# A decoder layer on one core: the opening reordered in halves, with x stored to DRAM later

## The chip, the cores and the metric

The kernel runs on one core of a Trainium2 chip, as one program of some 51,000 instructions. Its time is the device time of one execution in microseconds (us). A core has five engines that run their own instruction streams: TensorE (PE in the profile, with PEld for its weight loads), VectorE (DVE), ScalarE (ACT), GpSimd (POOL) and SyncE (SP). SP computes nothing; its queue, and POOL's, hold the instructions that start transfers between DRAM and the on-chip memory. Each engine takes its instructions in order, and one that waits holds up those behind it. Results of TensorE go to banks of PSUM, from where VectorE or ScalarE read them.

## The reference

One layer (DEPTH is 1) of a decoder over 1024 prompt rows and 8 x 4 sample rows, 1056 rows of 1024 values, all f32. A conditioning vector c for each of nine sequences (the prompt and eight samples) gives nine model vectors of 1024, three for each sublayer: shift, scale and gate.

```python
mod = jax.nn.silu(c) @ ada_w + ada_b                       # ada_w: 1024 x 9216
sh1, sc1, gt1, sh2, sc2, gt2, sh3, sc3, gt3 = jnp.split(mod, 9, axis=-1)
h = rms_norm(x, norm_ffn1) * (1 + sc1) + sh1
a, b = split(h @ ffn1_w_in, 2)                             # ffn1_w_in: 1024 x 5632
x = x + 0.5 * gt1 * ((silu(a) * b) @ ffn1_w_out)           # first FFN, D_FF = 2816
h = rms_norm(x, norm_mix) * (1 + sc2) + sh2
x = x + gt2 * token_mixer(h)                               # two branches: attention, retention
h = rms_norm(x, norm_ffn2) * (1 + sc3) + sh3
x = x + 0.5 * gt3 * swiglu_ffn2(h)
y = rms_norm(x, norm_final)
```

What the first FFN needs before its first product: x, transposed, and two of the nine vectors, sc1 (vector 1) and sh1 (vector 0).

## The kernel before

**Layout.** Activations are held transposed, 128 values of the model dimension to a tile and rows along it: X is 8 tiles (k = 0 to 7) by 1056 columns. The columns are worked in three row blocks of 352 (`rb` 0, 1, 2). Products are made with f32 accuracy from two rounded parts: `split` writes a high part with ScalarE (L183) and the remainder with VectorE (L193), and `mm3` makes three matmuls for each k (high by high, high by low, low by high: L242, L243, L244). One output tile for one row block, a `unit`, is thus 24 matmuls of 352 columns; a pair of units (`pa`, `pb`) makes one tile of the gated FFN.

**Weights.** A `W` pool has `raw` buffers of 512 KB for loads (`wr`, asked for on SP at L211) and `parts` pairs of buffers for the split parts. `w` (2 raw, 4 pairs) serves the FFN; `w0` (4 raw, 2 pairs) serves the model vectors in the opening, and a small pool of one each serves the other seven vectors, done beside the FFN (`more`).

**Model vectors.** `ada` makes vectors in the order it is given. A vector is made in halves of 512 (`u`), a half from four pieces of 256 x 512 of `ada_w` (`kq`; in the trace their tiles are `ada_0` to `ada_3`, the numbers of vector and half being left out). With the condition vectors as the stationary operand PE makes 18 (or 9) x 512 results in `adap`; ScalarE copies them to `ab` (L420), one matmul with `pick` or the identity turns them (L390), and VectorE adds the bias and makes the scale (L393, L395). Vector 1 (the scale) is marked `whole`: its pieces go to PE as plain f32, without a split. Vector 0 (the shift) and the rest are split.

**The opening**, in program order: the identity and constants; on SP the tables `cm` and `pgt`, the seven vectors of `vec` (bias and gains) and the conditions `c9`; their transposes; the four lambda vectors `lv` and the lambda of the attention; x by nine blocks of rows, each loaded by POOL's queue into `xn` (3 buffers, L751), transposed by eight PE transposes (L756) and copied to X by ScalarE and VectorE (L757); the sum of squares of row block 0; vector 1, then vector 0; and then the norm of row block 0, which writes `hh` and `hl`, the two parts of h, for k = 0 to 7 (L456, L460 to L465). Only then the first FFN: `ffn_plain` works three tile pairs in the order (tile 0, rb 0), (1, 0), (0, 1), (1, 1), (0, 2), (1, 2), (2, 0..2), with the norm of row block 1 traced after (0, 0), and `entry` after (0, 1): the norm of row block 2 and, by `keep1`, three stores of X to `xd` in DRAM, on POOL's queue (L769). After that the memory of X is given to the sums of a seven-product scheme (`sums`, L519 on), in which the other 19 tile pairs run (`ffn_seven`); X is read back from `xd` much later.

**Who orders.** The program order is not the order on the engines. A planner takes the traced instructions and issues on each engine the earliest in program order that is ready by its own estimates of time, and the result is fixed in the program. So a load whose buffer is free, or a store whose columns are written, can go out far ahead of its place. `step` ties the PE part of side work behind the last matmul traced.

Of the kernel before, what the change touches and what calls it, by code (L numbers as in the profile page):

```python
# [20 lines left out]
P = 128  # L21
# [84 lines left out]
def build(tc, i):  # L106
# [41 lines left out]
    def aux_ps(name):  # L148
        return banks[0][1].tile([P, 512], F32, tag="aux", name=name, bufs=banks[0][3])
# [132 lines left out]

    vT = cp.tile([P, 113], F32, name="vT")
    cs = cp.tile([P, KT, 18], F32R, name="cs")
    csf = cp.tile([P, KT, 9], F32, name="csf")
    with tc.tile_pool(name="init", bufs=1) as ip:
        vec = ip.tile([P, P], F32, name="vec")
        o = 0
        for n, r in (("ada_b", 72), ("norm_ffn1", 8), ("norm_mix", 8), ("norm_ffn2", 8), ("norm_final", 8),
                     ("ret_norm_g", 8), ("subln_g", 1)):  # L290
            src = i[n] if n == "norm_final" else i[n][0]
            ld(out=vec[o:o + r, :], in_=src.rearrange("(r p) -> r p", p=P))
            o += r
        pv = aux_ps("pv")
        T.transpose(pv[:, :113], vec[:113, :], ident[:113, :113])
        V.tensor_copy(out=vT[:], in_=pv[:, :113])
        c9 = ip.tile([9, D], F32, name="c9")
        ld(out=c9[0:1, :], in_=i["c_prompt"])
        ld(out=c9[1:9, :], in_=i["c_sample"])
        pc = aux_ps("pc")  # L300
        for k in range(KT):
            T.transpose(pc[:, k * 16:k * 16 + 9], c9[:, k * P:(k + 1) * P], ident[:9, :9])
        S.activation(csf[:], pc[:, :128].rearrange("p (k v) -> p k v", v=16)[:, :, :9], AF.Silu)
        split(cs[:, :, 0:9], cs[:, :, 9:18], csf[:])
    gff1, gmix, gff2, gfin, gret = (vT[:, 72 + 8 * j:80 + 8 * j] for j in range(5))
    subg = cp.tile([P, 1], F32, name="subg")
    V.tensor_scalar(out=subg[:], in0=vT[:, 112:113], scalar1=(1.0 - LAM_INIT) * 0.5, scalar2=None, op0=ALU.mult)
    retg = cp.tile([P, KT], F32, name="retg")
    V.tensor_scalar(out=retg[:], in0=gret, scalar1=0.25, scalar2=None, op0=ALU.mult)

    nlam = cp.tile([P, 1], F32, name="nlam")
    with tc.tile_pool(name="lam", bufs=1) as lp:
        lv = lp.tile([P, 4, 64], F32, name="lv")
        for j, n in enumerate(("lam_q1", "lam_k1", "lam_q2", "lam_k2")):
            ld(out=lv[:, j, :], in_=i[n][0].partition_broadcast(P))
# [11 lines left out]
    rsq = pool(root, "rsq")  # L327
# [50 lines left out]
    def ada(w, vectors):  # L378


        todo = [(v, u, kq) for v in vectors for u in range(2) for kq in range(4)]

        def load(n):
            (j, _, _, whole), u, kq = todo[n]
            c0 = j * D + u * 512
            return (w.load if whole else w.get)(i["ada_w"][0][kq * 256:(kq + 1) * 256, c0:c0 + 512], 2, 512, f"ada{j}_{u}_{kq}")

        def finish(pa, j, kind, g, whole, u):
            pt, t = pa[:, 512:], mods[j]
            T.matmul(pt[:, :36], ab[:], quarter(0) if whole else pick[:], start=True, stop=True)  # L390
# [9 lines left out]

        nxt, ready = load(0), None
        yield
        for n, ((j, kind, g, whole), u, kq) in enumerate(todo):
            if ready:
                finish(*ready)
                ready = None
            if kq == 0:
                m = 9 if whole else 18
                if u == 0:
                    mods[j] = (xp if j < 5 else cp).tile([P, KT, 9], F32, name=f"mod{j}")  # L410
                pa = big_ps(f"adap{j}_{u}")
            for k in range(2):
                for q, ww in enumerate((nxt,) if whole else nxt):
                    T.matmul(pa[:m, :512], (csf if whole else cs)[:, kq * 2 + k, :], ww[:, k, :],
                             start=(kq == 0 and k == 0 and q == 0), stop=(kq == 3 and k == 1 and (whole or q == 1)))
            if n + 1 < len(todo):
                nxt = load(n + 1)
            if kq == 3:
                for q in range(4):
                    S.copy(out=ab[32 * q:32 * q + m, :], in_=pa[:m, q * P:(q + 1) * P])  # L420
                ready = (pa, j, kind, g, whole, u)
            yield
# [15 lines left out]
    def norm(tp, X, rb, mods, gs, sh, tt=None):  # L438
# [14 lines left out]
        for k in range(KT):  # L453
            t = (tt or tp).tile([P, RB], F32, tag="t", name=f"nt{rb}_{k}", bufs=4)
# [29 lines left out]
    def ffn_plain(w, tp, win, fts, lead, pre, back=iter(()), more=iter(()), quiet=0):  # L484


        ws = {}
        for q, rb in [(q, rb) for q0 in range(0, len(fts), lead) for rb in range(NRB)
                      for q in range(q0, min(q0 + lead, len(fts)))]:
            ft = fts[q]  # L490
            if rb == 0:
                ws[q] = (w.get(win[:, ft * P:(ft + 1) * P], 8, P, f"wa{ft}"),
                         w.get(win[:, DFF + ft * P:DFF + (ft + 1) * P], 8, P, f"wb{ft}"))
            pa = unit(ws[q][0], rb, f"pa{ft}_{rb}")
            pb = unit(ws[q][1], rb, f"pb{ft}_{rb}")
# [235 lines left out]
    lower = ExitStack()  # L731
    w = W(lower, 2, 4)
    bridge = []
    with ExitStack() as sc, ExitStack() as sb_:
# [8 lines left out]
        tp = pool(sc, "t1")  # L743
        with ExitStack() as s2:
            xq = pool(s2, "xn")
            w0 = W(s2, 4, 2)
            for rt in range(9):
# [3 lines left out]
                st(out=xn[:n, :], in_=src)  # L751
                for hf in range(2):
                    pt = mm_ps(f"xt{rt}_{hf}")
                    for q in range(4):
# [4 lines left out]
            todo = norm(tn, X, 0, mods, 1, 0, tp)  # L759
            next(todo)  # L760
            run(ada(w0, [(1, "scale", gff1, True), (0, "shift", None, False)]))
            run(todo)
        w2 = W(sc, 1, 1)

        more = ada(w2, [(2, "half", None, False), (4, "scale", gmix, False), (3, "shift", None, False), (5, "gate", None, False),
                        (7, "scale", gff2, False), (6, "shift", None, False), (8, "half", None, False)])

# [25 lines left out]
        win1 = i["ffn1_w_in"][0]  # L793
        todo = back()
        ffn_plain(w, tp, win1, [0, 1, 2], LEAD, {(0, 0): norm(tn, X, 1, mods, 1, 0, tp), (PQ, 1): entry()}, todo, more, LEAD)
# [868 lines left out]
```

## Time and profile before

| | us |
|---|---|
| median of 3 executions | 3089.32 |
| the three | 3077.48, 3091.77, 3089.32 |
| the profiled execution, its own time | 3076.16 |
| its span in the profile | 3074.4 |
| granted TensorE clock, mean over the span | 0.987 |
| PE busy over the span | 2955.1 |

The profile is one execution. Each row of it names an engine, a line of the kernel, an operation and the tiles out<-in, with a start, a duration and, in brackets, how long the engine stood before it and what released it. Rows with xN are N instructions merged. A PE row's duration includes its run through the array, so following matmuls overlap, and a busy PE is not a PE at its peak. SPq and POOLq rows, and POOL rows with DMA, are the issue of a transfer, not the transfer. The DMA share is that of 16 engines.

### The profile page before, as it was taken

What the parts mean: (1) busy time and instruction counts of PE and PEld (TensorE: products, weight loads), DVE (VectorE), ACT (ScalarE), POOL (GpSimd) and SP (SyncE); (2) the same over time, 40 slices, a digit from 0 to 9 for tenths busy, and PEclk for the clock granted to TensorE, in tenths of its full rate; (3) what the DMA queues carried; (4) which work ended last, traced back from release to release, by engine and by line L of the source; (5) the groups of instructions that cost most, each with busy time, mean ns of one, the idle gap of its engine ahead of it and who ended that gap; (6) DMA issues with size and microseconds to landing.
All of it is one profiled execution on the core that took longest, in us unless ns stands there. A gap on an engine that the chain in (4) does not pass through costs nothing.

```text
span 3074.4 us, 51401 instructions
## 1 busy us (share of the span) xinstructions
PE 2955.1 (96%) x20167; PEld 2827.7 (92%) x20167; DVE 1969.2 (64%) x3823; ACT 1319.1 (43%) x2580; POOL 544.1 (18%) x722
## 2 busy tenths in 40 slices
PE   6999999999999999999999999998999999999998
PEld 2999999999999999988899998997898999999997
DVE  4875665665556666657666777676659655556546
ACT  5554444422234243336555555554545433333212
POOL 2200000000132322313233332332023000000002
PEclk8999999999999999999999999999999999999998
DMA  7143334653131322223222221225651222226311
GB/s 280 52 135 118 121 119 120 205 168 117 59 98 63 103 73 89 84 70 119 64 63 71 66 76 58 83 74 173 208 156 40 88 74 84 77 74 221 103 51 57
DMA packets 278732, 319.29 MB, mean 104 GB/s; under 512 B 15568, under 2 KB 224049, under 8 KB 278490
## 3 DMA queue, kind: packets, MB, share of 16 engines
q1 hardware_dynamic: 253418, 232.83, 24.9%
q0 software_dynamic: 25072, 83.18, 7.3%
q8 instruction: 158, 2.59, 0.3%
q14 instruction: 84, 0.69, 0.1%
HBM read 240.00 MB, written 75.96 MB: 103 GB/s over the span
## 4 chain that ended last, share of the span: by engine, by line
PE 35%; DVE 7%; issue 4%; ACT 3%; DMA 3%; POOL 1%; SPq 0%; DVEq 0%; ACTq 0%; POOLq 0%
PE po L244 3%; PE po L242 3%; PE po L243 3%; PE x L242 2%; PE x L243 2%; PE x L244 2%; PE q L243 1%; PE q L242 1%; PE q L244 1%; PE gp L242 1%; PE gp L244 1%; PE gp L243 1%; ACT P L1331 1%; DVE mx L1329 1%; DMA m<-md 1%
## 5 line engine op out<-in xcount | busy, mean ns | idle before, releaser
L242 PE MATMUL x<-hh,c 128*128 128x264 f32 x624 | 177.7, 285 | 3.3 <-DVE p L616 1.4
L242 PE MATMUL x<-gh,c 128*128 128x264 f32 x624 | 178.3, 286 | 0.6 <-ACT u L612 0.6
L193 DVE TENSOR_TENSOR c<-s,c 128x512 fp32r<-128x512 f32 x156 | 107.6, 690 | 111.1 <-ACT c L183 107.0
L243 PE MATMUL x<-hl,c 128*128 128x264 f32 x624 | 177.8, 285 | 0.3 <-DVE hl L193 0.3
L243 PE MATMUL x<-gl,c 128*128 128x264 f32 x624 | 177.7, 285 | 0.0
L244 PE MATMUL x<-hh,c 128*128 128x264 f32 x624 | 176.8, 284 | 0.8 <-DVE c L193 0.8
L244 PE MATMUL x<-gh,c 128*128 128x264 f32 x624 | 177.3, 284 | 0.0
L1331 ACT ACTIVATE P<-s,mx 128x256 f32<-128x256 f32 (+7 forms) x128 | 94.2, 739 | 136.7 <-DVE mx L1329 130.1
L475 DVE SCALAR_TENSOR_TENSOR Z<-po,mod,Z 128x352 f32<-128x352 f32 (+3 forms) x176 | 96.5, 554 | 87.3 <-PE po L244 86.6
L475 DVE SCALAR_TENSOR_TENSOR X<-po,mod,X 128x352 f32<-128x352 f32 (+3 forms) x152 | 82.0, 549 | 85.6 <-PE po L244 85.5
L625 POOL DMA_DIRECT2D gd<-p x39 | 21.1, 542 | 614.8 <-DVE p L620 614.8
L183 ACT ACTIVATE c<-s 128x512 fp32r<-128x512 f32 x156 | 97.5, 626 | 70.2 <-issue 35.1
L242 PEld LDWEIGHTS x<-hh,c 128*128 128x128 f32 x624 | 117.4, 188 | 4.7 <-DVE p L616 1.6
L242 PEld LDWEIGHTS x<-gh,c 128*128 128x128 f32 x624 | 117.4, 188 | 3.3 <-ACT u L612 0.9
L244 PEld LDWEIGHTS x<-hh,c 128*128 128x128 f32 x624 | 117.4, 188 | 1.2 <-DVE c L193 1.0
L243 PEld LDWEIGHTS x<-gl,c 128*128 128x128 f32 x624 | 117.3, 188 | 0.9
L243 PEld LDWEIGHTS x<-hl,c 128*128 128x128 f32 x624 | 117.4, 188 | 0.6 <-DVE hl L193 0.5
L244 PEld LDWEIGHTS x<-gh,c 128*128 128x128 f32 x624 | 117.4, 188 | 0.2
L242 PE MATMUL po<-hh,wo_1h 128*128 128x352 f32 (+1 forms) x328 | 105.7, 323 | 0.0
L243 PE MATMUL po<-hl,wo_1h 128*128 128x352 f32 (+1 forms) x328 | 104.2, 318 | 0.0
L244 PE MATMUL po<-hh,wo_1l 128*128 128x352 f32 (+1 forms) x328 | 103.8, 318 | 0.0
L242 PE MATMUL po<-hh,wo_0h 128*128 128x352 f32 (+1 forms) x328 | 103.5, 316 | 0.0
(1445 smaller groups left out, 11122.2 us busy)
## 6 DMA issues: line engine op xcount, KB each, us to landing
gr<-gd SPq DMA_DIRECT2D x40, 528.0 KB
gd<-u POOLq DMA_DIRECT2D x39, 264.0 KB, 2.3
gd<-p POOLq DMA_DIRECT2D x39, 264.0 KB, 2.3
ada_0r<-ada_w SPq DMA_DIRECT2D x18, 512.0 KB
ada_1r<-ada_w SPq DMA_DIRECT2D x18, 512.0 KB
ada_2r<-ada_w SPq DMA_DIRECT2D x18, 512.0 KB
ada_3r<-ada_w SPq DMA_DIRECT2D x18, 512.0 KB
st<-state_ret SPq DMA_DIRECT2D x32, 256.0 KB
```

The source lines that it names most:

```text
L183: S.activation(out, in_, AF.Copy, scale=scale)
L193: (eng or V).tensor_tensor(out=l, in0=src, in1=f(h), op=ALU.subtract)
L242: T.matmul(out, wh, xh, start=first and j == 0, stop=False, **kw)
L243: T.matmul(out, wh, xl, start=False, stop=False, **kw)
L244: behind[0] = T.matmul(out, wl_, xh, start=False, stop=last and j == n - 1, **kw).ins
L475: V.scalar_tensor_tensor(out=x[k][:, c0:c0 + n], in0=p_[:, :n], scalar=gt[:, k, 0:1], in1=x[k][:, c0:c0 + n], op0=ALU.mult, op1=ALU.add)
L625: st(out=gd[ft][:, :HR], in_=p1[:])
L1329: V.tensor_reduce(out=mx[:, :n], in_=sv[:, :, :wd], op=ALU.max, axis=AX.X, negate=True)
L1331: S.activation(pr[c][:, :wd], sv[:, j, :wd], AF.Exp, bias=mx[:, j:j + 1], accum_out=sums[c][:, qb:qb + 1])
```

## The change

The opening is cut and reordered; the FFN and everything behind it keep their order.

- `c9`, the conditions, is loaded first; then `first()` starts the generator of the model vectors, which asks for four pieces of `ada_w`; only then come the seven vectors and `cm`. `pgt` and the lambda part move into `lambdas`, run behind the FFN's pair (1, 0).
- Vectors 1 and 0 are made by halves: first half of 1, first half of 0, then the two second halves. All 16 pieces are split; `whole` is gone.
- x comes in three parts: rows 0 to 2 before the model vectors, by POOL's queue as before; rows 3 to 5 after the first half of the norm, by SP's queue; rows 6 to 8 behind the pair (1, 0), by SP's queue.
- The norm of row block 0 stops at k = 4. The first pair's first 12 + 12 matmuls (k = 0 to 3) are traced between its halves, the first weight pair (`wa0`, `wb0`) just before.
- The three stores of X to `xd` are issued by SP's queue instead of POOL's; their place in the program, in `entry`, stays.

The core of the diff:

```diff
-    ld(out=cm[:], in_=i["t_main"][:, :C_N0])
...
-    ld(out=pgt[:], in_=i["page_table"].rearrange("b n -> (b n)").unsqueeze(0))
...
+    lower = ExitStack()
+    w = W(lower, 2, 4)
+    sc, s2 = ExitStack(), ExitStack()
+    tp = pool(sc, "t1")
+    xq = pool(s2, "xn")
+    w0 = W(s2, 4, 2)
+
+    def opening(first):
+        with tc.tile_pool(name="init", bufs=1, side="right") as ip:
+            c9 = ip.tile([9, D], F32, name="c9")
+            ld(out=c9[0:1, :], in_=i["c_prompt"])
+            ld(out=c9[1:9, :], in_=i["c_sample"])
+            first()
+            vec = ip.tile([P, P], F32, name="vec")
...
+            ld(out=cm[:], in_=i["t_main"][:, :C_N0])
...
+    def lambdas():
+        ld(out=pgt[:], in_=i["page_table"].rearrange("b n -> (b n)").unsqueeze(0))
+        lp = pool(sc, "lam")
...
-    def ada(w, vectors):
-        todo = [(v, u, kq) for v in vectors for u in range(2) for kq in range(4)]
+    def ada(w, vectors, halves_first=False, ahead=0):
+        todo = [(v, u, kq) for v, u in ([(v, u) for u in range(2) for v in vectors] if halves_first else
+                                        [(v, u) for v in vectors for u in range(2)]) for kq in range(4)]
+        raws = {}
+        def load(n, part=True):
...
+            if n not in raws:
+                raws[n] = w.load(i["ada_w"][0][kq * 256:(kq + 1) * 256, c0:c0 + 512], 2, 512, name)
+            if part:
+                h, l = w.out(2, 512, name)
+                split(h[:], l[:], raws.pop(n)[:], eng=w.eng)
+                return h, l
...
+        for n in range(ahead):
+            load(n, False)
         nxt, ready = load(0), None
...
         for k in range(KT):
+            if halves and k == 4:
+                yield
...
-            for rt in range(9):
-                st(out=xn[:n, :], in_=src)
-            run(ada(w0, [(1, "scale", gff1, True), (0, "shift", None, False)]))
+        a0 = ada(w0, [(1, "scale", gff1), (0, "shift", None)], True, 4)
+        opening(lambda: next(a0))
...
+        run(rows_in(range(3), st, mm_ps))
+        todo = norm(tn, X, 0, mods, 1, 0, tp, True)
+        next(todo)
+        for _ in range(8):
+            next(a0)
+        got = {0: gated(w, win1, 0)}
+        next(a0)
+        next(todo)
+        begun = {(0, 0): units(got[0], 0, 0)}
+        for u in begun[0, 0]:
+            next(u)
+        run(rows_in(range(3, 6), ld, aux_ps))
+        run(a0)
+        run(todo)
+        def rest_in():
+            yield from rows_in(range(6, 9), ld, aux_ps)
+            s2.close()
+            lambdas()
...
             for rb in range(NRB):
-                keep1(X, rb, st)
+                keep1(X, rb, ld)
...
-        ffn_plain(w, tp, win1, [0, 1, 2], LEAD, {(0, 0): norm(tn, X, 1, mods, 1, 0, tp), (PQ, 1): entry()}, todo, more, LEAD)
+        ffn_plain(w, tp, win1, [0, 1, 2], LEAD, {(0, 0): norm(tn, X, 1, mods, 1, 0, tp), (1, 0): rest_in(), (PQ, 1): entry()},
+                  todo, more, LEAD, begun, got)
```

`rows_in` is the old loop over blocks of rows with the queue and the PSUM pool as arguments; `gated` and `units` are the old loads and units of a tile pair; `later` delays the pool and the generator of the other seven vectors until they are first stepped.

More of the change, by code (lines that the diff above doesn't have):

```diff
@@ L285, in build @@
     csf = cp.tile([P, KT, 9], F32, name="csf")
[L286 to L304, printed above, removed]
@@ L305, in build @@
-    gff1, gmix, gff2, gfin, gret = (vT[:, 72 + 8 * j:80 + 8 * j] for j in range(5))
[L306 to L312, printed above, removed]
+    subg = cp.tile([P, 1], F32, name="subg")
@@ L375, in quarter, with finish @@
         return ident[:].rearrange("p (q x) -> p q x", x=32)[:, :, o:o + 9]
-    def ada(w, vectors):
-        todo = [(v, u, kq) for v in vectors for u in range(2) for kq in range(4)]
[L383 to L388, printed above, removed]
+    def ada(w, vectors, halves_first=False, ahead=0):
[3 more added lines that the diff above has]
+        def load(n, part=True):
+            (j, _, _), u, kq = todo[n]
+            c0, name = j * D + u * 512, f"ada{j}_{u}_{kq}"
+            if n not in raws:
[4 more added lines that the diff above has]
+                return h, l
+        def finish(pa, j, kind, g, u):
             pt, t = pa[:, 512:], mods[j]
-            T.matmul(pt[:, :36], ab[:], quarter(0) if whole else pick[:], start=True, stop=True)
+            T.matmul(pt[:, :36], ab[:], pick[:], start=True, stop=True)
             tv = t[:, 4 * u:4 * u + 4, :]
@@ L399, in finish @@
                 V.tensor_scalar(out=tv, in0=tv, scalar1=0.5, scalar2=None, op0=ALU.mult)
+        for n in range(ahead):
+            load(n, False)
         nxt, ready = load(0), None
         yield
-        for n, ((j, kind, g, whole), u, kq) in enumerate(todo):
+        for n, ((j, kind, g), u, kq) in enumerate(todo):
             if ready:
@@ L412, in ada @@
             for k in range(2):
-                for q, ww in enumerate((nxt,) if whole else nxt):
-                    T.matmul(pa[:m, :512], (csf if whole else cs)[:, kq * 2 + k, :], ww[:, k, :],
-                             start=(kq == 0 and k == 0 and q == 0), stop=(kq == 3 and k == 1 and (whole or q == 1)))
+                for q, ww in enumerate(nxt):
+                    T.matmul(pa[:18, :512], cs[:, kq * 2 + k, :], ww[:, k, :],
+                             start=(kq == 0 and k == 0 and q == 0), stop=(kq == 3 and k == 1 and q == 1))
             if n + 1 < len(todo):
@@ L419, in ada @@
                 for q in range(4):
-                    S.copy(out=ab[32 * q:32 * q + m, :], in_=pa[:m, q * P:(q + 1) * P])
-                ready = (pa, j, kind, g, whole, u)
+                    S.copy(out=ab[32 * q:32 * q + 18, :], in_=pa[:18, q * P:(q + 1) * P])
+                ready = (pa, j, kind, g, u)
             yield
@@ L490, in ffn_plain @@
             ft = fts[q]
[L491 to L495, printed above, removed]
+            if rb == 0 and q not in ws:
+                ws[q] = gated(w, win, ft)
+            pa, pb = (run(u) for u in begun.get((q, rb)) or units(ws[q], ft, rb))
             for _ in range((q, rb) == (quiet - 1, 2) if q < quiet else 2 - rb % 2):
@@ L742, in build, with rows_in @@
         tn = pool(xs1, "n1", side="right")
[L743 to L746, printed above, removed]
-            for rt in range(9):
+        def rows_in(rts, eng, ps):
+            for rt in rts:
                 n = P if rt < 8 else NS
@@ L758, in build, with later @@
                                                       in_=pt[:].rearrange("p (k c) -> p k c", c=P)[:, :, :n])
-            todo = norm(tn, X, 0, mods, 1, 0, tp)
-            next(todo)
-            run(ada(w0, [(1, "scale", gff1, True), (0, "shift", None, False)]))
[L762 to L766, printed above, removed]
+                yield
+        win1 = i["ffn1_w_in"][0]
+        run(rows_in(range(3), st, mm_ps))
[16 more added lines that the diff above has]
+            lambdas()
+        def later():
+            yield from ada(W(sc, 1, 1), [(2, "half", None), (4, "scale", gmix), (3, "shift", None), (5, "gate", None),
+                                         (7, "scale", gff2), (6, "shift", None), (8, "half", None)])
+        more = later()
         def keep1(X, rb, eng):
```

40 lines of the change are left out of this document (30 added, 10 removed).

## The prediction

> **What bounds the kernel now.** I read the busy totals first, then the same totals by stretches of the span, then the opening in order of time, on SP's queue and on the engines that it feeds.
>
> The page's first part:
>
> ```profile
> PE 2955.1 (96%) x20167; PEld 2827.7 (92%) x20167; DVE 1969.2 (64%) x3823; ACT 1319.1 (43%) x2580; POOL 544.1 (18%) x722
> ```
>
> Busy time by stretch (us and count of PE, PEld, DVE, ACT, POOL; granted clock; DMA share; GB/s):
>
> ```profile
> 0.00:80.00 80.00, 51.12 (x185) 24.34 (x185) 39.26 (x61) 40.35 (x77) 20.14 (x29) 0.87 0.76 269
> 80.00:180.00 100.00, 96.93 (x618) 90.35 (x618) 90.18 (x145) 52.85 (x92) 16.21 (x19) 1.00 0.25 76
> ...
> 180.00:3074.00 2894.00, 2807.08 (x19368) 2712.98 (x19367) 1839.74 (x3619) 1225.91 (x2412) 507.75 (x674) 0.99 0.32 100
> ```
>
> TensorE bounds the kernel as a whole, and nothing in the change touches what it does after the opening. In the first 80 us it is short of work: 29 us idle, and 185 matmuls where the next 100 us hold 618. So the change is worth what it takes off the opening, less what comes back between 80 and 180 us, where VectorE has only 100 - 90.18 = 9.8 us free.
>
> What the opening waits for, in stretches of 5 us (same columns):
>
> ```profile
> 0.00:5.00 5.00, 0.00 (x0) 0.00 (x0) 0.50 (x3) 1.28 (x1) 2.44 (x9) 1.00 0.50 143
> ...
> 10.00:15.00 5.00, 5.00 (x21) 2.94 (x22) 1.05 (x3) 0.98 (x3) 0.53 (x1) 1.00 0.33 116
> ...
> 45.00:50.00 5.00, 4.79 (x12) 0.82 (x9) 2.82 (x7) 2.43 (x4) 0.43 (x1) 1.00 1.07 403
> 50.00:55.00 5.00, 0.00 (x0) 0.00 (x0) 2.56 (x3) 1.62 (x4) 0.49 (x1) 0.91 1.04 403
> 55.00:60.00 5.00, 3.64 (x8) 1.75 (x9) 3.77 (x6) 3.20 (x8) 1.39 (x2) 0.50 0.61 158
> ...
> 70.00:75.00 5.00, 5.00 (x14) 2.45 (x13) 3.04 (x5) 2.46 (x4) 0.00 (x0) 0.54 0.00 1
> ```
>
> The transfers are the limit: at 45 to 55 us they run at 403 GB/s, all 16 engines busy, while PE has nothing from 50 to 55. There is a hole early (116 GB/s at 10 to 15 us). Its cause stands on SP's queue, and the stores of x, which nobody needs yet, on POOL's (start, duration):
>
> ```profile
> 6.14 0.47 SPq L211 DMA_DIRECT2D ada_1r<-ada_w  x1
> 10.91 0.35 SPq L315 DMA_DIRECT2D lv<-lam_q  x1
> ...
> 12.72 0.43 SPq L211 DMA_DIRECT2D ada_2r<-ada_w  x1
> ...
> 28.50 0.96 POOL L769 DMA_DIRECT2D xd<-X  x1
> ...
> 34.21 0.91 POOL L769 DMA_DIRECT2D xd<-X  x1
> ...
> 42.07 0.91 POOL L769 DMA_DIRECT2D xd<-X  x1
> ...
> 79.64 0.20 DVE L393 TENSOR_TENSOR mod<-adap,vT 128x36 f32<-128x36 f32 x1 [1.15 <-PE adap L390]
> ...
> 83.27 0.43 PE L243 MATMUL pa<-hl,wa0h 128*128 128x352 f32 x1 [0.25 <-DVE hl L465]
> 83.53 0.33 PE L244 MATMUL pa<-hh,wa0l 128*128 128x352 f32 x1
> 83.69 0.32 PE L242 MATMUL pa<-hh,wa0h 128*128 128x352 f32 x1
> ```
>
> SP stood from 6.61 to 10.91 us before the lambda vectors, with two ada pieces behind them. The last of the four halves of the two model vectors is ready at 79.64 + 0.20 = 79.84 us, and from 83.3 us PE runs unbroken, a matmul every 0.16 us. I call the first moment M; the sum is about where M goes.
>
> **The change part by part.** (1) *Bytes ahead of M.* From the DMA part of the trace, sizes and counts of the opening:
>
> ```profile
> xd<-X POOLq DMA_DIRECT2D x3, 1408.0 KB, 9.6
> xn<-x_prompt POOLq DMA_DIRECT2D x8, 512.0 KB, 6.5
> ...
> wa0r<-ffn_w_in SPq DMA_DIRECT2D x1, 512.0 KB
> ...
> xn<-x_sample POOLq DMA_DIRECT2D x1, 128.0 KB, 5.4
> ```
>
> Before M lie 16 ada pieces (8 for each vector, 512 KB as the others), x with 8 x 512 + 128, four w pieces of 512, and about 106 KB of small vectors: 8192 + 4224 + 2048 + 106 = 14570 KB = 14.9 MB. The three stores are 4224 KB = 4.3 MB more. The first 5 us moved 143 x 5 = 0.72 MB, which at 403 GB/s is 1.8 us, so transfers start in effect at 3.2 us. With the stores behind M the last piece lands at 3.2 + 14.9 / 0.403 = 40.2 us; with all of them ahead, at 3.2 + 19.2 / 0.403 = 50.8 us. The change puts the conditions and four ada pieces ahead of the seven vectors and moves pgt and the lambda loads far back, so I count the early hole as closed.
>
> By "DMA: Bandwidth & Descriptors" of the Trainium skill (section Bandwidth, Where 436 GB/s comes from) loads from HBM are held to about 358 GB/s for a core, not 403; as an estimate from that figure the two landings would be 44.9 and 56.8 us, each 5 to 6 us later than above. This trace's 403 over 10 us, with loads and stores mixed, is above it, and I keep 403.
>
> From landing to M the trace has the last piece of before, and a buffer's turn:
>
> ```profile
> 44.67 0.37 SPq L211 DMA_DIRECT2D ada_0r<-ada_w  x1
> ...
> 53.35 1.06 ACT L183 ACTIVATE ada_0h<-ada_0r 128x1024 fp32r<-128x1024 f32 x1 [3.49 <-DMA ada_0r<-ada_w]
> ...
> 54.44 1.23 DVE L193 TENSOR_TENSOR ada_0l<-ada_0r,ada_0h 128x1024 fp32r<-128x1024 f32 x1 [2.44 <-ACT ada_0h L183]
> 55.70 0.37 SPq L211 DMA_DIRECT2D ada_0r<-ada_w  x1
> ...
> 73.59 1.06 ACT L183 ACTIVATE ada_3h<-ada_3r 128x1024 fp32r<-128x1024 f32 x1 [0.70 <-PE adap L414]
> ...
> 74.68 1.23 DVE L193 TENSOR_TENSOR ada_3l<-ada_3r,ada_3h 128x1024 fp32r<-128x1024 f32 x1 [0.53 <-ACT ada_3h L183]
> ```
>
> The last split starts at 73.59, M is at 79.84: 6.25 us. So M by bytes is 46.4 us (stores behind) to 57.1 us (stores ahead).
>
> (2) *Slots.* The ada loads still have four raw buffers. One was issued at 44.67, its data was there at 53.35, its split ended at 55.67, and the buffer was asked for again at 55.70: 11.0 us a turn. Now all 16 pieces go through splits, four turns. The first ends about when four pieces and half as much x have landed and been split, 3.2 + 3.7 / 0.403 + 2.3 = 14.7 us; three more turns give 47.7, and from a split's end (74.68 + 1.23 = 75.91) to M is 3.9: M = 51.6 us. The turn was measured under full transfers, so it is no floor and no ceiling.
>
> I take M = 52, near the slots' value, since the stores' place is open: they went out on POOL as soon as their columns were there, long ahead of their line in the program, and SP's queue is ordered by the same planner. Gain at M: 79.84 - 52 = 28 us; ends 33 and 23.
>
> (3) *Eight more splits.* The scale vector's eight pieces went to PE as plain f32. Now each costs ACT 1.06 and DVE 1.23 us: ACT +8.5, DVE +9.8. DVE's work up to M becomes 39.3 + 9.8 = 49.1 us, to be done between about 8 us (the first piece, 0.5 MB from 3.2 us on at half the rate with x beside it, lands near 6, and ACT's half comes first) and 52, in 44 us. It worked at 39.3 of 80 before. Taking 75% of the 44 us, 33 are done and 16 go behind M; at 90% it is 9.5, at 60% 22.7. That is not all urgent (squares and copies of later rows, the second weight pair). Behind M, DVE has the 9.8 us free, most of it in one wait for PE that such work can fill:
>
> ```profile
> 100.72 0.52 DVE L500 TENSOR_TENSOR silu<-silu,pb 128x352 f32<-128x352 f32 x1 [6.37 <-PE pb L244]
> ```
>
> So 16 - 9.8 = 6 us come back as stalls of PE (0 to 13 at the ends). From M on the order of the FFN is the old one.
>
> (4) *First half before the second.* Blocks k 0 to 3 of the first row block and their 24 matmuls may run while the second halves load. Before, PE had also done scattered matmuls of that kind by 83 us (it took them out of order from 73 us on), so I count nothing; at most 24 matmuls more are ahead, 3.8 us of gain.
>
> (5) *At nothing.* The 16 f32 matmuls become 32 split ones on a PE that idles 29 us here; if they did bind, M would move past 52 and that is inside the 57. x rows 3 to 8 go from POOL's to SP's queue and their transposes into the idle PE. If the 24 transposes of rows 6 to 8 fell behind M they would be on PE's path, by the group below 24 x 0.309 = 7 us at most. The seven vectors and the eps columns come after four ada pieces, still long before the first mod result of any half needs them; if they were late, that result would be late by as much. The lambda part's Exp sits in the FFN then: two table loads at worst, 1.28 us each, on an ACT that is busy 52.85 of 100 us. POOL loses nine issues; nobody waits for them. The stores must have read X before the sums overwrite it (113 us before): even issued at the first row block's end, about 72, they need 4.3 / 0.403 = 10.7 us, done by 83 against 113 - 28 = 85, with DMA at share 0.04 then.
>
> ```profile
> L756 PE MATMUL xt<-ident,xn 128*128 128x128 f32 (+1 forms) x72 | 11.4, 309 | 4.4 <-DMA xn<-x_prompt 2.7 <-DVE X L757 1.4 <-ACT X L757 0.2
> ...
> 41.13 1.28 ACT L361 ACT_TABLE_LOAD   x1
> ...
> 113.11 0.69 DVE L519 TENSOR_TENSOR t<-hh 128x528 f32<-128x528 f32 x1
> ```
>
> ```profile
> 70.00:120.00 50.00, 47.58 (x261) 41.11 (x260) 37.63 (x61) 28.63 (x52) 16.00 (x16) 0.95 0.04 15
> ```
>
> **Sum.** -28 (M) + 6 (DVE) = -22 us. The profiled execution took 3076.2 us by its own time (span 3074.4): 3054. The runs shown stand at 3077, 3089 and 3092, so the median 3089.3 is 13 above the profiled one, and most executions will be there: 3089.3 - 22 = 3067.
>
> **Rivals.** *VectorE becomes the bound* (0.20): utilisation stays near 60% since each split waits for ACT and for the transfer; 13 us come back, and with M at 57 the gain is 23 - 13 = 10: 3079. For it: DVE is at 90% from 80 to 180 us already. Against: its early idling was for transfers, which now come sooner.
>
> *The stores do not move* (0.14), the part "x to DRAM later" being undone by the planner: M at 57.1, gain 22.7 - 6 = 17: 3073. For it: the issues at 28.50, 34.21 and 42.07, far ahead of their line.
>
> *Quicker* (0.10): M at 46.4 and the backlog all in DVE's gaps: gain 33: 3056.
>
> *Slower: SP's queue blocks* (0.08). It works in order, and now holds x rows 3 to 8, whose buffers come free by PE's transposes, and stores that wait for copies of X, among the ada loads. One such wait cost 4.3 us before (6.61 to 10.91). To end slower by 0.5% they must take 22 + 15 = 37 us, nine such waits in a row, each with the transfers idle: 3089 + 16 = 3105. Against: from 15 us on the transfers were full in spite of waits, so a wait costs only when the ring runs dry.
>
> **How the numbers follow.** The forecast itself has 0.48; its own range is 3058 to 3076 (gain 13 to 31). The bound that tells a change is 0.5%, 15.4 us. Faster: 0.41 of the forecast, 0.08 of the 0.14, the 0.10, and 0.03 of VectorE's case: 0.62. Slower: 0.07. Same: 0.31. The range leaves out the slow rival and the best of the quick one, and takes in that a median may fall with the low run (12 below): 3042 to 3087.
>
> **What would show it.** Right: four ada issues by about 4 us; no hole at 10 to 15 us; the last of the four first mod results near 52 us; PE unbroken from about 55. Stores: the three xd issues on SP; ahead of the last ada piece they cost what (1) says. DVE: its busy time up to M near 33 us and the wait of 6.37 us filled. Wrong if M stays past 65 us, or if PE idles over 10 us between M and M + 100.

## The result and the profile after

The changed kernel takes 3070.19 us (median of 10 runs, 3059.52 to 3077.88) and the kernel before 3084.81 (median of 10, 3077.2 to 3091.77). The ratio is 0.9949, interval 0.9937 to 0.996: faster by 0.5%. The interval lies below 1 as a whole, but on both sides of the 0.995 from which the prediction counts a kernel as faster. The profiled execution took 3059.52 us (span 3057.8) against 3076.16 (3074.4). So 14.6 us are gained by the medians and 16.6 by the profiled spans, where the prediction had 22. Its median of 3067 came out nearer than its gain, and that is luck: the gain was put 7.4 us too high, and the 10 runs of the kernel before have a median 4.5 us below that of the three runs it started from.

The busy totals and the busy times by stretch of the kernel after (us and count of PE, PEld, DVE, ACT, POOL; granted clock; DMA share; GB/s):

```profile
PE 2941.8 (96%) x20167; PEld 2823.6 (92%) x20167; DVE 1978.1 (65%) x3831; ACT 1327.3 (43%) x2589; POOL 538.3 (18%) x713
...
0.00:60.00 60.00, 37.50 (x168) 21.40 (x169) 40.30 (x54) 40.45 (x67) 11.50 (x17) 0.94 0.83 279
60.00:160.00 100.00, 94.98 (x595) 87.00 (x594) 93.04 (x152) 59.34 (x108) 19.18 (x22) 1.00 0.37 117
...
5.00:10.00 5.00, 1.97 (x8) 1.57 (x8) 1.23 (x1) 1.32 (x2) 0.00 (x0) 1.00 1.04 414
10.00:15.00 5.00, 2.04 (x8) 1.30 (x8) 1.46 (x2) 3.12 (x5) 0.00 (x0) 1.00 0.67 220
...
5.00:65.00 60.00, 40.58 (x184) 23.78 (x184) 45.13 (x57) 43.77 (x78) 9.99 (x9) 0.94 0.88 296
20.00:65.00 45.00, 31.84 (x149) 18.37 (x147) 39.28 (x46) 36.59 (x69) 9.99 (x9) 0.92 0.88 291
...
30.00:65.00 35.00, 26.68 (x136) 16.23 (x133) 32.78 (x37) 29.53 (x54) 7.06 (x6) 0.99 0.91 311
```

The stretch in which PE is short of work has shrunk from 80 to 60 us. The transfers reach 414 GB/s at 5 to 10 us and run at 291 from 20 to 65, with a share of 0.88: not full as before, but not far from it. VectorE is nearly full: 32.78 of 35 us from 30 to 65, with ACT at 29.53.

The four opening mod results on DVE (the last one ends M), and the sixth store of an FFN block's product on POOL. That store closes two FFN blocks over all three row blocks. I call its issue E; the expectations call it the last gd store of the first row block. Kernel after, then E of the kernel before:

```profile
26.71 0.19 DVE L412 TENSOR_TENSOR mod<-adap,vT 128x36 f32<-128x36 f32 x1 [0.92 <-PE adap L409]
...
38.84 0.13 DVE L412 TENSOR_TENSOR mod<-adap,vT 128x36 f32<-128x36 f32 x1
...
52.55 0.20 DVE L412 TENSOR_TENSOR mod<-adap,vT 128x36 f32<-128x36 f32 x1
...
61.76 0.18 DVE L412 TENSOR_TENSOR mod<-adap,vT 128x36 f32<-128x36 f32 x1
...
113.21 0.54 POOL L529 DMA_DIRECT2D gd<-silu  x1 [6.81 <-DVE silu L528]
```

```profile
128.70 0.54 POOL L501 DMA_DIRECT2D gd<-silu  x1 [6.80 <-DVE silu L500]
```

M went from 79.84 to 61.94: 17.9 us, not 28. E went from 128.70 to 113.21: 15.5. So 48.86 us from M to E became 51.27, and 2.4 us came back. Behind E the two profiled runs take 2945.7 and 2944.6 us: all but 1.1 us of the difference lies ahead of E. For the experiments E is the yardstick. The time is not, for one run each: from E to the end the kernels of the experiments take 2948 to 2961 us, with mean granted clocks of 0.986 to 0.990, and that spread hides differences of 2 us.

### The profile page after: what moved, and what is told of

Read it like the earlier page. It is cut to its first block, busy times and chain, and to the rows that moved or that the text cites. A ratio compares the mean times of both kernels' runs of the same rounds, so it can differ in the third digit from the quotient of the medians.

```text
span 3057.8 us, 51405 instructions
## 1 busy us (share of the span) xinstructions
PE 2941.8 (96%) x20167; PEld 2823.6 (92%) x20167; DVE 1978.1 (65%) x3831; ACT 1327.3 (43%) x2589; POOL 538.3 (18%) x713
## 4 chain that ended last, share of the span: by engine, by line
PE 36%; DVE 7%; ACT 3%; issue 3%; DMA 3%; POOL 1%; DVEq 0%; ACTq 0%; POOLq 0%; SPq 0%
PE po L241 3%; PE po L239 3%; PE po L240 3%; PE x L239 2%; PE x L240 2%; PE x L241 2%; PE q L240 1%; PE q L239 1%; PE q L241 1%; PE gp L239 1%; PE gp L241 1%; PE gp L240 1%; DVE mx L1376 1%; PE wop L239 1%; ACT P L1378 1%
## 5 line engine op out<-in xcount | busy, mean ns | idle before, releaser
L180 ACT ACTIVATE hh<-gr 128x1056 fp32r<-128x1056 f32 (+1 forms) x48 | 47.6, 1010 | 130.1 <-PE po L241 62.3
```

The lines of the kernel that those rows point to most:

```text
L180: S.activation(out, in_, AF.Copy, scale=scale)
```

## The experiments

What could have set M at 61.94 instead of 52, and what took the 2.4 us:

- Q: SP's queue holds back the second round of pieces. B: bytes, the prediction's first step. S: the splits on ACT and DVE.
- L: the first half starts late and the rest follows. T: a half is a serial turn of PE, ACT and DVE (one accumulator, two pairs of split buffers, queues in order). W: VectorE and ACT are simply full.
- N, for the 2.4 us: the third row block's norm begins too late.

SP's queue in the kernel after, on which Q rests:

```profile
2.96 1.07 SPq L208 DMA_DIRECT2D ada_3r<-ada_w  x1
...
5.44 0.29 SPq L308 DMA_DIRECT2D vec<-norm_ffn  x1
6.69 0.27 SPq L308 DMA_DIRECT2D vec<-norm_final  x1
9.74 0.27 SPq L308 DMA_DIRECT2D vec<-ret_norm_g  x1
11.76 0.22 SPq L308 DMA_DIRECT2D vec<-subln_g  x1
13.21 0.36 SPq L310 DMA_DIRECT2D cm<-t_main  x1
13.68 0.39 SPq L208 DMA_DIRECT2D ada_0r<-ada_w  x1
...
50.40 1.84 SPq L816 DMA_DIRECT2D xd<-X  x2
```

The four pieces left by 4 us as predicted, but behind the fourth vector SP issues one at a time: three more vectors and `cm`, at 6.69, 9.74, 11.76 and 13.21. The trace names the landing of pieces 0, 1, 2 and 3 in turn as what released SP, each eight transfers before the one issued (ACT takes up piece 0 at 6.69 and piece 1 at 9.74). Whether the program or the chip sets this eight is not shown. The first buffer was free at 9.01, and its next load left at 13.68. This is the 220 GB/s hole at 10 to 15 us that the prediction counted as closed.

All results (us; half results 1 to 4 on DVE; M; E):

| kernel | 1 | 2 | 3 | 4 | M | E | E - M |
|---|---|---|---|---|---|---|---|
| before | 39.29 | 56.08 | 67.83 | 79.64 | 79.84 | 128.70 | 48.9 |
| after | 26.71 | 38.84 | 52.55 | 61.76 | 61.94 | 113.21 | 51.3 |
| e1 vectors by POOL | 24.12 | 35.87 | 52.46 | 61.90 | 62.10 | 116.81 | 54.7 |
| e2 half the splits on GpSimd | 28.14 | 39.23 | 61.16 | 72.44 | 72.6 | 126.95 | 54.3 |
| e3 scale vector unsplit | 27.13 | 36.83 | 52.68 | 60.17 | 60.37 | 110.92 | 50.6 |
| e4 stores by POOL | 24.03 | 34.73 | 51.88 | 60.63 | 60.83 | 116.28 | 55.5 |
| e5 conditions first | 27.25 | 37.44 | 51.74 | 62.00 | 62.20 | 113.59 | 51.4 |
| e6 third split pair | 28.18 | 37.54 | 49.97 | 62.59 | 62.79 | 116.05 | 53.3 |
| e7 no halves | 26.56 | 38.95 | 49.06 | 58.18 | 58.38 | 120.94 | 62.6 |
| e8 lambdas late | 26.93 | 39.70 | 55.05 | 64.33 | 64.53 | 115.86 | 51.3 |
| e9 second accumulator | 26.26 | 36.04 | 54.40 | 62.28 | 62.48 | 115.19 | 52.7 |
| e10 FFN behind third half | 26.81 | 39.40 | 49.72 | 63.29 | 63.47 | 116.80 | 53.3 |
| e11 e3 and e9 together | 25.68 | 35.95 | 50.48 | 58.01 | 58.21 | 111.61 | 53.4 |
| e12 e3, x rows early | 27.25 | 36.96 | 55.28 | 65.55 | 65.68 | 114.49 | 48.8 |

e8 shows how far an edit can shift things by the planner's order alone: M and E moved by 2.6 us with no edit ahead of M. A move of M or E of that size in one run says little.

**e1: the vectors off SP's queue.**

```
-                ld(out=vec[o:o + r, :], in_=src.rearrange("(r p) -> r p", p=P))
+                st(out=vec[o:o + r, :], in_=src.rearrange("(r p) -> r p", p=P))
-            ld(out=cm[:], in_=i["t_main"][:, :C_N0])
+            st(out=cm[:], in_=i["t_main"][:, :C_N0])
     (and x rows 0 to 2 are issued on POOL's queue ahead of them)
```

> The seven model-vector loads and cm go by POOL's queue, behind x rows 0 to 2 there; all else is the changed kernel, whose M (last of the four opening mod results) is at 61.9 us. Theory Q (SP's queue holds back the second round of ada pieces: eight transfers in flight at most, and the ninth waits for the first; the buffer of the first piece was free at 9.0 us and asked for again at 13.7): the second round is asked for from 9 us, no stretch under 250 GB/s between 10 and 25 us, M at 56 to 58. Theory S (ACT and DVE bound the opening with 16 splits beside the norm): the second round starts earlier too, but M moves by less than 2 us, 60 to 62.

The transfers of e1, same columns as above:

```profile
10.00:15.00 5.00, 2.01 (x8) 1.25 (x8) 1.46 (x2) 3.12 (x5) 1.02 (x2) 1.00 1.08 383
15.00:20.00 5.00, 4.41 (x16) 1.64 (x14) 4.05 (x4) 4.15 (x5) 0.00 (x0) 1.00 1.04 366
```

The hole is filled, the second round starts at 9.44 us, the first two results come 2.6 and 3.0 us earlier. The third does not move, M neither, and E is 3.6 later, for which no run has the cause. Q falls as what sets M. Time 3066.18 (before, for e1 to e4, 3075.61).

**e2: half the opening's splits to GpSimd.**

```
-                split(h[:], l[:], raws.pop(n)[:], eng=w.eng)
+                split(h[:], l[:], raws.pop(n)[:], eng=G if ahead and n % 2 else w.eng)
```

> Of the 16 opening ada pieces the odd ones get their remainder from GpSimd instead of VectorE: 8 x 1.22 us leave DVE's queue. Theory S with DVE as the bound: M from 61.9 to 54 to 58. Theory Q: M within 2 us of 61.9. If POOL's own time (three times DVE's or so) takes the place, M rises above 62.

Groups on POOL and PE's longest wait there, kernel e2:

```profile
L188 POOL TENSOR_TENSOR ada_3l<-ada_3r,ada_3h 128x1024 fp32r<-128x1024 f32 x4 | 13.7, 3434 | 9.9 <-ACT ada_3h L180 9.9
L188 POOL TENSOR_TENSOR ada_1l<-ada_1r,ada_1h 128x1024 fp32r<-128x1024 f32 x4 | 9.4, 2361 | 13.0 <-ACT ada_1h L180 13.0
...
PE adap L434 <- POOL ada_3l L188: 5.0, 3, 2.2
```

The last line is a wait: 5.0 us in three times, the longest 2.2. A remainder takes 2.4 and 3.4 us in the mean of the two groups instead of 1.2 on DVE, and PE waits for it. M 10.7 later, 3079.03 us. It says nothing for or against S, since POOL became the late one.

**e3: the scale vector without splits**, as plain f32 matmuls like before.

```
+                if ahead and j == 1:
+                    return (raws.pop(n),)
     (matmuls of csf with the raw piece, 9 rows instead of 18)
```

> Only the split of the scale vector is undone: its eight pieces go to PE as plain f32 as before the change, in the new order of halves. ACT loses 8.5 and DVE 9.8 us of the opening, PE's matmuls for them are as before. Theory S: M at 53 to 57. Theory Q: M within 2 us of 61.9, since the pieces are asked for no earlier. Rival: PE, slow in the opening, makes it later than 62.

This takes 8.5 us off ACT and 9.8 off DVE: DVE's 32.78 us at 30 to 65 become 27.32. M moves by 1.6 and E by 2.3, time 3062.7. So relieved of nearly 10 us of work on each of the two engines, the opening ends 2 us sooner, of the 10 that S was to explain. The test is not clean, since it loads PE in exchange: a plain piece takes PE 1.72 us (from 44.27 to 45.99 in e3), a split one 0.94 (52.80 to 53.74 in the kernel after), and PE goes from 26.68 to 29.98 of the 35 us and is now the fullest of the three.

**e4: the stores of x on POOL's queue.**

```
-                keep1(X, rb, ld)
+                keep1(X, rb, st)
```

> Only the queue of the three stores of X is undone (POOL instead of SP). Theory by bytes (the prediction's part 1): the stores go out as soon as their columns are written, 4.3 MB at 0.4 MB/us ahead of the last ada pieces, M later by 5 to 11 us (67 to 73). Theory S, with transfers at 281 GB/s on average and so not full: M later by less than 3 us.

The first two stores left at 21.81 and 45.02 us, ahead of the last pieces, as in the kernel before:

```profile
21.81 0.92 POOL L816 DMA_DIRECT2D xd<-X  x1 [18.38 <-DVE X L784]
45.02 0.93 POOL L816 DMA_DIRECT2D xd<-X  x1
```

M came 1.1 us earlier, not later: B falls, and for M "x to DRAM later" is worth nothing that shows. Time 3067.67. E is 3.1 later (E - M 55.5); the order of the work behind M changed too, and what the later stores are worth there stays open.

**e5: the conditions' Silu and split ahead of the first pieces.**

```
+            silu = S.activation(csf[:], pc..., AF.Silu)
+            split(cs[:, :, 0:9], cs[:, :, 9:18], csf[:])
+            with tc.issue_after(silu.ins):
+                first()
```

> Edit: the transposes, Silu and split of the conditions stand ahead of the first ada pieces' splits on ACT, so that PE's first half can begin near 9 us instead of 12.96. M (last of the four opening mod results) is 61.94 us in the changed kernel. Late start (theory L: the first half came 8 us late, and all later ones only follow it): all four results 3 to 4 us earlier, M near 58, the last gd store of the first row block from 113.2 to near 110, time 3 lower. Something between the second and the third half sets the third (theory T: the third result was at 52 us in all five kernels so far): first two results 2 to 4 us earlier, third stays at 52 within 1, M within 1.5 us of 61.9, the gd stores within 1.5.

PE's first half began at 10.21 instead of 12.96, and its result came at 27.25 instead of 26.71. Three rows of e5 show who took the 2.7 us (PE, DVE, ACT):

```profile
14.68 0.29 PE L318 MATMUL pv<-ident,vec 113*128 113x113 f32 x1 [1.16 <-DMA vec<-ret_norm_g]
...
15.01 0.28 DVE L319 COPY vT<-pv 128x113 f32<-128x113 f32 x1 [3.03 <-PE pv L318]
...
23.84 0.50 ACT L456 ACTIVATE sq<-X 128x352 f32<-128x352 f32 x1 [1.27 <-POOL acc L457]
```

The seven vectors, now behind the pieces, stand as one transpose in PE's queue and one copy in DVE's; the low part of piece 2, whose high part was ready at 13.03, comes on DVE behind that copy, at 16.17. At the other end the four copies that empty the accumulator (ACT, 22.33 to 25.14) wait behind squares of the norm that wait for POOL. An earlier start alone brings nothing, and L falls with e1 and e4 too, whose first results came 2.6 us earlier and whose M stayed within 1.1; time 3065.03 (before, for e5 to e8, 3083.89).

**e6: three pairs of split buffers, three raw ones.**

```
-    w0 = W(s2, 4, 2)
+    w0 = W(s2, 3, 3)
```

> Edit: three pairs of split buffers and three raw ones instead of two and four for the opening's ada pieces (the memory allows no more). ACT waited twice 4.0 us for PE to free a pair. If the pairs are what makes a half last 11.7 us (theory T, its buffer form), the later halves take 9 to 10 us and M comes at 55 to 58. If the raw buffers do (the prediction's slots), three of them make a turn of 4 pieces last 11 x 4/3 = 14.7 us and M comes at 66 to 72. If neither binds, M stays within 1.5 us of 61.9.

The third result comes 2.6 us earlier, the fourth 0.8 later: 12.6 us from the third to the fourth instead of 9.2. T asked for M at 55 to 58 and the prediction's slots, with three raw buffers, for 66 to 72: 62.79 is neither. The edit changes two things at once, and the raw buffer less can have cost what the pair gained. Time 3068.07.

**e7: no halves**, the scale vector whole and then the shift vector, as before the change.

```
-        a0 = ada(w0, [...], True, 4)
+        a0 = ada(w0, [...], False, 4)
-        for _ in range(8):
-            next(a0)
+        run(a0)
```

> Edit: the halves in the order of before (both halves of the scale vector, then both of the shift vector), all four ahead of the norm's and the FFN's first halves. Theory T, its order form (norm's first half on DVE and 24 FFN matmuls that wait for it stand between the second and third half on in-order queues): without them the third result comes at 47 to 49 and M at 56 to 58; PE then starts the FFN with nothing done, and the first gd store comes 0 to 4 us earlier or later than 70.1. If the order costs nothing, the third stays at 52 and M at 62, and the first gd store is later by the work that lay ahead: 24 matmuls of 0.16 us, 4 us, at 74.

M is 3.6 us earlier, and E 7.7 later, time 3074.05. The norm of the second row block shows the main part (its reciprocal on DVE; e7, then after):

```profile
70.25 2.35 DVE L373 RECIPROCAL rrn<-rrn 128x352 f32<-128x352 f32 x1 [2.36 <-ACT rrn L372]
```

```profile
61.87 2.33 DVE L373 RECIPROCAL rrn<-rrn 128x352 f32<-128x352 f32 x1
```

With halves, the second row block's squares are done ahead of M (its rows 3 to 5 are traced between the halves) and its reciprocal stands at M. Without them it comes 11.9 us behind M, and E - M is 62.6 instead of 51.3. The FFN's matmuls make a smaller difference: 17 are done at M in e7 and 29 in the kernel after, and 12 at 0.16 us are 1.9 us of the 11.3. Ten more transposes of x behind M take PE another 1.1 (2.79 us against 1.66). What the late norm alone costs no run isolates, so that it is the main part is argued. The halves, with what they let in between them, put M off and are worth half of the whole gain at E (7.7 of 15.5).

**e8: the lambda part behind the FFN's first blocks.**

```
             s2.close()
-            lambdas()
...
+        lambdas()
         ffn_seven(...)
```

> Edit: the lambda part's loads, Exp and arithmetic go behind the opening FFN's first seven blocks instead of into its first row block. M stays at 61.9 within 0.5. If ACT's two table loads (1.28 each, at 82.02 and 83.54 us) are what delays norm 2 and with it the first row block's later blocks, the last gd store comes at 110.7 to 112 instead of 113.2 and the time is 1 to 2 lower. If VectorE's backlog is it (the prediction's step 3), the gd stores stay within 0.4 us.

E - M is 51.3 as before the edit: no sign that ACT's two table loads take any of the 2.4 us. M itself came 2.6 us later although nothing ahead of it was edited; the order that the planner wrote changed. Time 3067.93.

**e9: accumulators of their own for the shift vector's halves.**

```
-                pa = big_ps(f"adap{j}_{u}")
+                pa = aux_ps(f"adap{j}_{u}") if ahead and not g else big_ps(f"adap{j}_{u}")
```

> Edit: the shift vector's two halves accumulate in PSUM banks of their own (with the result of the picking matmul in another bank), so that PE need not wait for the mod result of the half before. Theory T (a half is a serial turn: PE's first matmul of the next half waits for the mod result of the last one, 27.59 us behind 26.71 and 52.80 behind 52.55 in the changed kernel, while the split weights lay ready from 22.85 and from 51.41): the second half starts near 23 and the fourth near 51.5, results 2 and 4 come 2 to 4 us earlier, M near 58 to 60, the last gd store of the first row block at 110 to 112 instead of 113.2. Rival W (no turn: VectorE and ACT are simply full, 94% and 84% busy from 30 to 65 us, and whatever comes earlier is taken from something else): M may move by up to 3 us, but the last gd store stays within 1 us of 113.2.

The second result comes 2.8 us earlier, the third 1.9 later. PE's queue in e9:

```profile
41.22 0.40 PE L434 MATMUL adap<-ada_2h,cs 128*18 128x512 f32 x1 [0.30 <-ACT ada_2h L180]
...
49.50 0.39 PE L434 MATMUL adap<-ada_2l,cs 128*18 128x512 f32 x1
```

Between these two matmuls of one piece stand the 24 of the FFN's first half, which wait for DVE and POOL. In the kernel after they stand between two pieces of that half (41.64 to 48.19). T asked for M at 58 to 60 and E at 110 to 112, W for E within 1 us of 113.2: M at 62.48 and E at 115.19 are neither. Time 3065.79 (before, for e9 to e11, 3086.62).

**e10: the FFN's first half behind the third half.**

```
-        for _ in range(8):
+        for _ in range(12):
             next(a0)
```

> Edit: the first half of the first row block's norm and FFN (k 0 to 3, 24 matmuls that wait for VectorE's and POOL's remainders, at 42 to 48 us on PE in the changed kernel) is traced behind the third half's pieces instead of ahead of them. Theory T, its order form: the third result comes near 48 instead of 52.55 and M near 57 to 58, and since the 24 matmuls still run while the fourth half loads, the last gd store comes 3 to 4 us earlier, near 109.5. Rival W: what the halves gain the FFN loses; the third result and M come earlier, but fewer FFN matmuls stand done at M and the last gd store stays within 1.5 us of 113.2 or is later, as without halves (120.9).

The third result comes 2.8 us earlier, the fourth 1.5 later, E 3.6 later: what the half gained the FFN lost, as W had it; M, which both had earlier, came later, and T had E near 109.5. Time 3067.04.

**e11: e3 and e9 together.**

> Edit: two of the edits together, the scale vector's pieces unsplit and the shift vector's halves in accumulators of their own. Alone the first moved M by 1.6 and the last gd store by 2.3 us (to 110.9). Theory T: both gains add, M near 56 to 58, the last gd store near 107 to 109, time 5 to 6 us below the changed kernel's on the same chip. Rival W (VectorE and ACT full): the first has already taken 9.8 and 8.5 us from them, so the accumulator has room to work and gains the full 2 to 4 here even if it gained nothing alone. If a third limit (PE, with four f32 passes for each plain matmul, or the loads) binds instead, M stays at 60.4 and the last gd store at 110.9, within 1.

M 58.21, 3.7 earlier: here the accumulator gives 2.2 us on top of e3, as T and W both allow. E moves by 1.6 only, where T asked for 4 to 6, and is 0.7 later than in e3. Time 3074.34, with E to end at 2961 us against 2945: single times don't rank these kernels.

**e12: e3 with rows 6 to 8 of x loaded and turned behind rows 3 to 5.**

```
-        run(rows_in(range(3, 6), ld, aux_ps))
+        run(rows_in(range(3, 9), ld, aux_ps))
         run(a0)
...
-            yield from rows_in(range(6, 9), ld, aux_ps)
+            yield
```

> Edit on top of the unsplit scale vector (e3): rows 6 to 8 of x (the last of the third row block) are loaded and turned right behind rows 3 to 5, ahead of the second halves, instead of behind two FFN blocks. In the changed kernel the last of these rows reached X at 76.6 us, 15 us behind M, and with it came the third block's squares (76.9 to 81.6), its reciprocal (85.42) and its blocks, for which PE waits between 91 and 103 us (0.4 to 0.6 us a time; PE busy 7.76 of 10 us from 90 to 100 where it is full before and behind). Theory N (the 2.4 us that come back behind M are the third row block's norm, begun too late): the reciprocal comes before 78 us, PE is busy at least 19.4 of the 20 us from 90 to 110 (17.3 in the changed kernel, 17.5 in e3), and the last gd store comes at 108 to 109.5 instead of 110.9 in e3 and 113.2; time 17 to 20 below the kernel before, ratio 0.9935 to 0.9945. Rival W (VectorE is full from 90 to 120 us, 29.8 of 30): its work is the same, so what is taken from that stretch lands on it elsewhere, ahead of M too: M goes from 60.4 to 62 or 63, and the last gd store stays within 1 us of 110.9. If rows 6 to 8 on SP's queue hold back the second halves' pieces, M goes past 63 and the last gd store past 112.

From M to E, in before, after and e12 (columns as above):

```profile
79.84:128.70 48.86, 46.63 (x279) 43.94 (x278) 40.30 (x65) 26.87 (x48) 14.05 (x16) 1.00 0.11 34
```

```profile
61.94:113.21 51.27, 47.63 (x286) 44.22 (x285) 45.74 (x78) 33.08 (x60) 17.02 (x18) 1.00 0.35 111
```

```profile
65.68:114.49 48.81, 47.24 (x275) 45.40 (x276) 43.81 (x75) 31.07 (x54) 13.76 (x16) 0.97 0.30 96
```

With the rows early E - M is 48.8, that of the kernel before. PE idles 2.2 us on the way in the kernel before, 3.6 in the kernel after and 1.6 in e12, and the 14 transposes of x that PE has there in the kernel after (1.66 us) stand ahead of M again. That supports the late rows as the cause, N in its wider sense. It doesn't single out the third block's norm: its reciprocal came at 83.85 us and not before 78, and the kernel before has a wait of PE of this kind too (8.02 of 10 us busy from 110 to 120). And a shorter way from M is in part M's own delay: M came 5.3 us later than in e3. The rows' transposes, copies and squares now stand ahead of the last two halves; SP's queue, which the expectation names for an M past 63, is not seen to do it, since from 17.6 us to M no row of PE, ACT or DVE is released by a transfer. In ten runs e12 takes 3071.38 us against 3081.28, ratio 0.9962, interval 0.9948 to 0.9976: no better than the change itself. No run gave a version that is shown to beat it; e3's E, 2.3 us earlier, is below what these runs can tell in time.

## Why the prediction was right, and where not

**Right.** The direction, the place (all but 1.1 us ahead of E), the four issues by 4 us, PE idle for 4.7 of the 100 us behind M where 10 was the limit, and the stores behind the last piece. The side (faster) by the median; the interval takes in the bound. What gained the 17.9 us at M is not shown part by part: the unsplit scale vector (e3), the stores on POOL (e4) and the order without halves (e7) each left M no later, so the early pieces and x in three parts remain, and no run undoes those.

**Bytes ahead of M: wrong as the limit.** M by bytes was 46.4 to 57.1; it came at 61.94, with transfers at 291 GB/s, and with stores (e4) and earlier loads (e1) that put M off by nothing. In the kernel after the last row of PE, ACT or DVE ahead of M that a transfer releases is this one:

```profile
9.74 1.06 ACT L180 ACTIVATE ada_1h<-ada_1r 128x1024 fp32r<-128x1024 f32 x1 [1.99 <-DMA ada_1r<-ada_w]
```

From there on no engine is seen to stand for a piece. The prediction could have seen it: its row at 73.59 us, from which it counts 6.25 us to M, waits for PE and not for a landing, and from 70 to 75 us its transfers have a share of 0.00. The early hole stayed, by SP's eight transfers in flight. As to the 358 GB/s of the Trainium skill ("DMA: Bandwidth & Descriptors", Where 436 GB/s comes from): the stretch at 5 to 10 us holds loads alone and ran at 414, so the trace stays above it.

**Slots: mis-sized by 10 us.** This is the step that failed. It had the first result at 18.6 us (14.7, and the 3.9 from a split's end) and three turns of 11.0. The first result came at 26.9, 8.3 later; the turns took 12.1, 13.7 and 9.2 us, 2.0 more in all. Of the 8.3 us, 6.4 lie ahead of the end of the fourth split (21.12 us, not 14.7) and 1.9 behind it.

The four loads were nearly in time: the fourth had landed by 13.21, where 3.2 + 3.7 / 0.403 gives 12.4. (These 3.7 MB are four pieces and three blocks of x, 2.1 + 1.6; "half as much x" would be 3.1.) The sum let the splits follow the loads and put their waits at nothing. There are two pairs of split buffers, and the third split had to wait until PE had worked off a pair; PE could not begin before 12.96, when the conditions were split; and the fourth remainder stood on DVE behind the vectors' and x's copies:

```profile
14.46 1.06 ACT L180 ACTIVATE ada_2h<-ada_2r 128x1024 fp32r<-128x1024 f32 x1 [1.82 <-PE adap L434]
...
19.91 1.21 DVE L190 TENSOR_TENSOR ada_3l<-ada_3r,ada_3h 128x1024 fp32r<-128x1024 f32 x1
```

Taking one of these away does not bring the result forward: with the conditions first (e5) it came at 27.25, with a third pair (e6) at 28.18. Behind the split's end the result passes PE, four copies on ACT, PE and DVE, on queues in which the norm's squares stand ahead. PE's waits for these copies, kernel after:

```profile
26.03 0.64 PE L409 MATMUL adap<-pick,ab 128*128 128x36 f32 x2 [3.99 <-ACT ab L440]
...
37.52 0.41 PE L409 MATMUL adap<-pick,ab 128*128 128x36 f32 x2 [1.52 <-ACT ab L440]
...
52.10 0.41 PE L409 MATMUL adap<-pick,ab 128*128 128x36 f32 x2 [1.87 <-ACT ab L440]
```

The turn of 11.7 us in the mean is near the 11.0, but not for the sum's reason: 11.0 was a raw buffer's turn under full transfers, and no row shows buffers or transfers setting the pace here. No split waits for its load after 9.74 in the kernel after, and e6, with three raw buffers, has a mean of 11.5 where the buffers' rule gives 14.7. They may still act through the planner's own estimates, which fix the order; no run tests that.

No single limit accounts for the 10 us. No edit on one suspect moved M forward by more than 3.6 us (e7), two together by 3.7 (e11), and what one half gained, the next lost (e6, e9, e10). Engines that are all nearly full, with queues in order, would do that, a mix of T and W. But T missed its numbers in e6, e9, e10 and e11, W its own in e9, and no run took either away as a whole. So the cause of the 10 us is argued and stays open, and so does whether 52 us can be reached.

**Eight more splits: right in place, wrong in kind.** 6 us were to come back, 2.4 did. By 52 us DVE had done 32.6 us, as the sum had it (33). But M was not there: DVE did 42.2 us by M (45.13 from 5 to 65 us, less the 3.06 behind M, and 0.17 ahead of 5 us), so most of the backlog stood ahead of M in its queue. And what came back was hardly the splits: without the eight more e3 has an E - M of 50.6, and with the rows early as well e12 has 48.8. It goes with x rows 6 to 8, whose transposes and norm moved behind M, a step counted at nothing but for its transposes.

**First half before the second: counted at nothing, worth 7.7 us** (e7). For the matmuls, which the step had in mind, nothing was nearly right: 29 were done at M against 21 in the kernel before, 8 at 0.16 us. What it left out is the second row block's norm, which came ahead of M. Without halves the kernel lands on the numbers of the rival "VectorE becomes the bound": M 58.4, 13.7 back and 7.8 left, where that rival had M 57, 13 back and 10 left. That is chance: in e7 VectorE has 28.88 of the 35 us from 30 to 65, less than in the kernel after. A gain at M too large by 10, and one at nothing that was worth nearly 8, made the sum look better than its parts; the hit on the time is in part luck.

**At nothing.** The table loads cost nothing that shows (e8), as said. POOL's nine issues and the stores against the sums left no mark either, though no run tests them alone. The vectors behind the pieces were not free: they held SP's queue to 13.2 us, and e5 shows them holding PE and DVE as soon as the conditions no longer do.

## What to carry to other kernels

A sum from loads and buffer turns came out 10 us short for this opening: follow one result through every engine that it passes, and look at what stands ahead of it in each queue. A row that waits for another engine says nothing of when its data landed. With engines each 75 to 95% busy and in order, relieving two of them by nearly 10 us and loading a third gave 2. Judge an opening by a point behind it that all its work must have passed: M was 3.6 us earlier in a kernel that reached E 7.7 us later.

## What the runs showed of the hardware

GpSimd and VectorE slowed each other down. In the kernel after, three of VectorE's nt took 1.56 us alone and 2.84 beside two remainders on POOL; these took 1.15 us each, and one at 76.75 us, with VectorE idle, 0.94:

```profile
67.06 1.56 DVE L478 SCALAR_TENSOR_TENSOR nt<-X,mod,rrn 128x352 f32<-128x352 f32 x3
...
71.47 2.84 DVE L478 SCALAR_TENSOR_TENSOR nt<-X,mod,rrn 128x352 f32<-128x352 f32 x3
```

```profile
71.13 2.30 POOL L484 TENSOR_TENSOR hl<-nt,hh 128x352 fp32r<-128x352 f32 x2 [0.49 <-ACT hh L180]
...
76.75 0.94 POOL L484 TENSOR_TENSOR hl<-nt,hh 128x352 fp32r<-128x352 f32 x1 [0.15 <-ACT hh L180]
```

The Trainium skill states this sharing ("GPSIMD Engine Reference", Specifications: contention with VectorE's instructions that have two SBUF inputs); the trace agrees, with 0.52 us against 0.95 for one.

TensorE's granted clock fell behind an idle stretch of the opening. PE stood from 22.04 to 26.03 us waiting for ACT, and the next stretch has a clock of 0.50:

```profile
25.00:30.00 5.00, 3.88 (x9) 1.91 (x10) 2.53 (x5) 2.77 (x6) 1.10 (x2) 0.50 0.94 274
```

The second half's matmuls start 0.43 us apart there (28.96, 29.39) and 0.24 apart from 31.99 on. What this costs at M no run separates.

Between an edit and the order there is a planner: e8 moved M by 2.6 us with no edit ahead of M, and e11 took 16 us longer behind E than the kernel after. Whether its order or the granted clock (0.987 against 0.990) did that stays open.
